# Half-wide products that alternate between the two partition halves of their output

## The chip, the core and the metric

The kernel runs on one core of a Trainium2 chip. The metric is the device time of one execution in microseconds (us). The engines are named as the profile names them: PE (TensorE, the matrix products), PEld (its weight loads, which overlap PE), DVE (VectorE), ACT (ScalarE), POOL (GpSimd) and SP (SyncE, which issues most transfers).

## The reference, cut to what matters

Two blocks follow each other over 512 tokens of 1024 features. Block 1 has two mixers and two feed-forward layers; its second mixer holds a spatial gating and a causal "forgetting" attention, both with 8 heads of 64 features. Block 2 has two layers, each with three branches; branch c is a neighbourhood attention with 8 heads of 64 features, for 512 tokens and, in layer 0, also for 256 tokens of a context. All of it is in float32.

```python
# block 1, second mixer
mixed = jnp.einsum('gts,bnsgc->bntgc', w_causal, gv) + b_s.T[:, :, None]     # c: 64 features of a gating head
...
p = jax.nn.softmax(logits, axis=-1)
return jnp.einsum('bhqk,bhkd->bhqd', p.astype(v.dtype), v)                    # d: 64 features of a head
# block 2, branch c
return jnp.einsum('bhnqik,binkhd->bnqhd', p_loc, vr) + jnp.einsum('bhnqj,bjhd->bnqhd', p_ctx, vc)
...
y_cc = softmax_attn(na_h(cqc), na_h(ckc), na_h(cvc)).reshape(B, L, BR_W) * jax.nn.silu(czc)
```

## The kernel before

Features lie on partitions and tokens on the free axis. The projections are products of 128 weight columns with 512 or 256 tokens; each float32 weight is split into two parts (tiles `wh`, `wl`) and each operand into two (`H`, `L`), and three passes of the split type stand for one float32 product. Weights come in units of 128 columns through `wload`: a transfer on SP, a copy on ACT, a subtraction on DVE.

The 64-feature heads are treated in pairs (`hp` 0 and 1, the first and the second head of pair `j`). For a tile `t` of 128 queries `attend` makes the scores (`mm_stack`), the softmax on DVE and ACT, the transposes of the probabilities (PE, `P<-C,..` in the trace, C being the constants with the identity), their copy out of PSUM into `pT` (ACT), and then the product with the head's values. That last product has 64 output features: head 0 writes partitions 0 to 63 of its PSUM tile, head 1 writes partitions 64 to 127. It is a plain float32 product with 128 rows, 64 weight columns and 128 moving columns, one for each tile `n` of keys, summed in PSUM. In this text these are the half-wide products; one that writes partitions 0 to 63 belongs to half 0, the others to half 1. The spatial gating (`mixed`) has the same shape: head `2 j` in half 0, head `2 j + 1` in half 1, four products each. There are 400 half-wide products: 112 in block 1 (80 of the attention, 32 of the gating), 160 in layer 0 of block 2, 128 in layer 1. A float32 product leaves two matmul records and two weight-load records in the trace, so there are 800 records.

The order on the engines isn't that of the code: the class `Order` records the instructions, and `flush` issues them by a list schedule, engine by engine, from planned costs. An engine takes the first written instruction that can start. So the half-wide products of one head are placed one by one, in between projections and transposes, and stretches of them of any length and of either half arise. All instructions of the kernel are issued at one line of `flush`, so the trace has them all at L465 and they are told apart by their tiles and shapes. In the names P is PSUM; `t` tiles belong to block 1 and `s` tiles to block 2; `P<-t,t` with the shape 128*64 is a half-wide product of block 1, `P<-s,s` with 128*64 one of block 2.

Of the kernel before, what the change touches and what calls it, by code (L numbers as in the profile page):

```python
# [12 lines left out]
AF = mybir.ActivationFunctionType  # L13
# [14 lines left out]
# ---------------------------------------------------------------- host layout  # L28
def _units(w):
    """[K, N] -> [N/128, 128, K/128, 128]: each 128-column unit contiguous."""  # L30
    k, n = w.shape
    return np.ascontiguousarray(w.reshape(k // 128, 128, n // 128, 128).transpose(2, 1, 0, 3))


def _halves(w):
    """[K, N] -> [2, 128, K/256, N]: a unit of N columns in two halves of K."""
    k, n = w.shape
    return np.ascontiguousarray(w.reshape(2, k // 256, 128, n).transpose(0, 2, 1, 3))


def _cols(v):
    """[.., C] -> [128, n]: a feature vector as partition columns, leading axes in order."""
    v = np.asarray(v)
    return v.reshape(-1, 128).T
# [17 lines left out]
def consts():  # L62
# [4 lines left out]
    # queries on partitions, keys on the free axis  # L67
    p.add("cmask", np.where(i[None, :] <= i[:, None], 0.0, NEG).astype(np.float32))
    # source s on partitions, target t on the free axis
# [7 lines left out]
def rope_tables():  # L77
    """[2, 128, 512]: cos and signed sin, a feature on each partition (two groups of 64)."""
# [3 lines left out]
    ang = np.concatenate([row[:, None] * inv, col[:, None] * inv], axis=-1)  # [T, 32]  # L82
# [10 lines left out]
def nbias(rpb):  # L93
    """[H, 15, 31] -> [H, 128, 768]: the bias of a block of 16 columns x 8 rows of queries
    against its window of 32 columns x 8 rows of keys, for the first, a middle and the last
    block; keys outside a query's own window get a constant."""
    out = []
    r = np.arange(8)
    for n in (0, 1, 3):
# [6 lines left out]
        b = rpb[:, ri[None, :, None, :], ci[:, None, :, None]]  # H, qc, rq, kc, rk  # L106
# [41 lines left out]
def layout(inputs):  # L148
# [28 lines left out]
    for l in range(2):  # L177
# [5 lines left out]
        # [8 m, 3 branches, 128, 4, 128]  # L183
# [6 lines left out]
# ---------------------------------------------------------------- issue order  # L190
# [9 lines left out]
class Order:  # L200
    """Records the instructions of a stretch of the kernel in the order they are written in, and
    issues them in the order of a list schedule: an engine takes the first written one of those
    that can start, given when operands arrive and slots of tile tags come free. Tile puts in the
    waits and the addresses."""

# [6 lines left out]
    # sets of function tables; the others are in all of them  # L212
# [3 lines left out]
    def __init__(self, tc, nc):  # L216
# [8 lines left out]
        self.tiles = {}   # name -> [tag, number]  # L225
        self.caps = {}    # tag -> slots
        self.made = {}    # tag -> tiles made
        self.clock = {e: 0.0 for e in self.LAG}
        self.dma = 0.0
        self.slots = {}   # tag -> times at which free slots came free  # L230
        self.held = {}    # tile -> tag, while it holds a slot
        self.done_at = {}  # tile -> end of its last issued instruction
        self.reset()

    def reset(self):
        self.ops = []
        self.floor = 0.0  # the earliest start of the next ones
        self.late = 0     # how many instructions later the next ones may come
        self.acc = {}
        self.last = {}  # L240

# [10 lines left out]
    # ---- recording  # L252
# [13 lines left out]

    def record(self, eng, op, f, a, k):
# [9 lines left out]
        i = len(self.ops)  # L277
        deps = {}
        if eng == "pe":
            # accumulation groups in a PSUM bank follow one another  # L280
            x = k["out"] if "out" in k else a[0]
            bank = (x.tensor.name, x.offset % (list(x.ap)[0][0] or 1) // 512)
            if k.get("start", True) and bank in self.last:
                deps[self.last[bank]] = False
# [26 lines left out]
        self.ops.append(dict(p=(i + self.late, i), r=self.floor, e=eng, s=self.SETS.get(a[2]) if eng == "act" and op == "activation" else None, f=f, a=a, k=k, d=deps, t=touched, c=self._cost(eng, op, a, k, aps, psum)))  # L311
# [37 lines left out]
    # ---- issue  # L349
    def flush(self, keep=()):  # L350
# [20 lines left out]
        # tiles of each tag that wait for a slot, in the order they were made  # L371
# [90 lines left out]
        with self.tc.manual_schedule():  # L462
            for i in order:
                o = ops[i]
                o["f"](*o["a"], **o["k"])  # L465
        self.reset()


def weave(*gens):
    """Runs generators, of (steps, generator) each, side by side in proportion to their lengths."""  # L470
# [8 lines left out]
def chain(*gens):  # L479
    """the same, one after another"""  # L480
# [6 lines left out]
# ---------------------------------------------------------------- the kernel  # L487
class Kern:
    WST = 3

    def __init__(self, ctx, tc, A, cat, vat):
# [15 lines left out]
        # the split operand of the projections, tokens of x first, then those of the context  # L507
# [23 lines left out]
    def pt(self, n=512, p=128):  # L531
        """a bank of PSUM"""
# [3 lines left out]
    def pts(self, n, p=128):  # L536
        """n columns over banks of PSUM: (tile, first column, columns)"""
        return [(self.pt(min(512, n - o), p), o, min(512, n - o)) for o in range(0, n, 512)]

    # ---- weights: loaded in 128-column units and split exactly into two float32r parts  # L540
# [16 lines left out]
    def mm3(self, ps, w, xh, xl, order=None, start=True, stop=True):  # L557
        """ps += w.T x over the k tiles of xh, xl (lists), as three float32r passes."""
# [8 lines left out]
    def tok4(self, src, tiles):  # L567
        """a projection of about 256 columns of each 128-column tile of H, L (their columns in
        `tiles`): the first tile, [128 tokens, tile, columns], with as many to a bank of PSUM as fit"""
# [20 lines left out]
    def stack(self, q, k, hp, new, nq, nk):  # L590
        """Operands on all 128 rows for the product of a head's 64 rows of q and k:
        [q hi; q hi], [q lo; q lo] against [k hi; k lo]."""
# [19 lines left out]
    # ---- 1/sqrt(v) for few columns  # L612
# [17 lines left out]
class Stream:  # L630
    """The running sum of squares of a residual stream's features, for n tokens."""
# [16 lines left out]
    def sums(self, p):  # L648
        """the sums, tokens on partitions, into columns of PSUM"""
# [7 lines left out]
    def spread(self, r, p):  # L657
        """a value for each token, on every partition, into PSUM"""
# [6 lines left out]
    def rstd(self):  # L665
        """1/rms of each token: on every partition, in PSUM, and with tokens on partitions"""
# [12 lines left out]
def block1(K, X, out, dbg, mods, B, es):  # L679
# [18 lines left out]
    def feed(m, g):  # L698
        """X[:, m] g as operand of the next projections, whose results get the factor 1/rms"""
# [10 lines left out]
    def proj(*src):  # L710
        """one or two units of 128 columns"""
# [7 lines left out]
    def scaled(p, R):  # L719
        """halves of a PSUM tile, each times R"""  # L720
# [5 lines left out]
    def gelu2(src, dst=None):  # L726
        """2 gelu(src), the tanh form."""
# [10 lines left out]
    def conv(p, wname, bname, j, taps, ntile):  # L738
        """causal depthwise convolution of a [128, T] tile"""
# [15 lines left out]
    def lru_rates():  # L755
        """4 softplus(-lambda) and its negative; half biases"""
# [24 lines left out]
    def even(first):  # L781
# [11 lines left out]
        for j in range(0, 4, 2):  # L793
            for j, p in zip((j, j + 1), scaled(proj(W[j], W[j + 1]) if j else pre, R)):
# [10 lines left out]
                # 1 - a^2 = tanh(z) (1 + a^2)  # L805
# [30 lines left out]
    def odd():  # L836
# [4 lines left out]
        # forget gates: negative running sum of log sigmoid, one row per head  # L841
# [27 lines left out]
        # spatial gating: gate half, token-major  # L869
# [13 lines left out]
        def mixed():  # L883
            # gt holds 2 gelu
# [13 lines left out]
            for j in range(4):  # L898
                m = K.pt(T)
                for q in range(2):  # L900
                    h = 2 * j + q
                    for n in range(4):
                        nc.tensor.matmul(m[64 * q:64 * q + 64, n * 128:(n + 1) * 128],
                                         lhsT=gt[n][:, h * 64:(h + 1) * 64], rhs=wt[h // 4][:, h % 4],
                                         start=True, stop=True)
                mx.append(t2())
# [5 lines left out]
        # forgetting attention, two heads at a time  # L912
# [37 lines left out]
        def attend(j):  # L950
            vt, st, cb, cm = heads.pop(j)
            o = K.pt(T)
            for t in range(4):
                q0, nk = t * 128, (t + 1) * 128
                for hp in range(2):
                    P0 = 64 * hp
# [22 lines left out]
                    pT = t2()  # L979
                    nc.scalar.activation(pT[:, :nk], tt[:, :nk], AF.Copy)  # L980
                    for n in range(t + 1):
# [847 lines left out]
```

## Time and profile before

| | |
|---|---|
| three runs | 2955.85, 2951.63, 2955.36 us; median 2955.36 us |
| span of the profiled execution, first to last instruction | 2953.9 us |
| PE busy | 2902.0 us (98% of the span) |
| DVE, ACT, POOL busy | 1889.7, 1256.5, 242.5 us (64%, 43%, 8%) |
| mean granted clock of PE | 0.994 of full speed |

The profiled execution's own time isn't listed apart from its span; the median of the runs lies 1.5 us above that span. A share of busy time is read with care on PE: its records overlap, since matmuls are pipelined. What a product costs PE is read from the distance between the starts of two that follow each other, or from the length of a row that merges many of them.

### The profile page before, as it was taken

How to read it: one execution, taken by the hardware profiler on the slowest of the kernel's cores; microseconds unless marked ns; L12 is line 12 of the kernel's file. 1: busy time of each engine (PE TensorE's matmuls, PEld its weight loads, DVE VectorE, ACT ScalarE, POOL GpSimd, SP SyncE). 2: the span in 40 equal slices, each digit the busy share in tenths (PEclk: the TensorE clock that was granted, in tenths of full speed). 3: DMA queues.
4: the chain of work that ended last, by engine and by line, in shares of the span. 5: the costliest groups of instructions: out<-in, count | busy, mean ns of one | idle time of the engine just before them, and what ended most of it. 6: DMA issues, size and time to landing. Idle time of an engine off the chain costs nothing.

```text
span 2953.9 us, 41015 instructions
## 1 busy us (share of the span) xinstructions
PE 2902.0 (98%) x15990; PEld 2458.0 (83%) x15990; DVE 1889.7 (64%) x3799; ACT 1256.5 (43%) x2400; POOL 242.5 (8%) x184
## 2 busy tenths in 40 slices
PE   9999999999999999999999999999999999999998
PEld 6888888887888888888888888888888888888887
DVE  7778687568885876556876763222475586765334
ACT  6344244454442444655555432222356554533223
POOL 1010000100100011001110210000300011110002
PEclk9999999999999999999999999999999999999999
DMA  4333433322334433111111111222422111222333
GB/s 153 126 119 120 145 132 108 118 81 72 127 109 146 144 91 127 47 63 44 37 45 58 54 61 54 68 65 67 136 79 82 37 58 44 73 72 68 100 93 104
DMA packets 94802, 260.58 MB, mean 88 GB/s; under 512 B 9608, under 2 KB 23304, under 8 KB 94608
## 3 DMA queue, kind: packets, MB, share of 16 engines
q1 hardware_dynamic: 94464, 257.96, 27.0%
q8 instruction: 125, 2.05, 0.3%
q14 instruction: 69, 0.57, 0.1%
q10 hardware_dynamic: 144, 0.00, 0.0%
HBM read 251.29 MB, written 6.64 MB: 87 GB/s over the span
## 4 chain that ended last, share of the span: by engine, by line
PE 93%; DVE 4%; ACT 1%; issue 1%; DMA 1%; POOL 0%; SPq 0%; POOLq 0%; ACTq 0%; DVEq 0%
PE P L465 93%; DVE s L465 2%; DVE wl L465 1%; ACT s L465 1%; DVE tn L465 1%; DVE t L465 0%; DMA s<-cmd 0%; POOL s L465 0%; ACT t L465 0%; ACT wh L465 0%; DMA V<-in_vec 0%; DMA t<-cd 0%; DVE L L465 0%; DMA ws<-in_w0in 0%; DMA cmd<-s 0%
## 5 line engine op out<-in xcount | busy, mean ns | idle before, releaser
L465 PE MATMUL P<-L,wh 128*128 128x512 f32 (+1 forms) x2936 | 1079.7, 368 | 3.7 <-DVE L L465 3.6
L465 PE MATMUL P<-H,wh 128*128 128x512 f32 (+1 forms) x2936 | 1078.4, 368 | 3.7 <-ACT s L465 1.6
L465 PE MATMUL P<-H,wl 128*128 128x512 f32 (+1 forms) x2936 | 1078.3, 367 | 3.3 <-DVE wl L465 3.3
L465 ACT ACTIVATE wh<-ws 128x1024 fp32r<-128x1024 f32 (+4 forms) x426 | 412.1, 968 | 926.2 <-PE P L465 836.9
L465 DVE TENSOR_TENSOR wl<-ws,wh 128x1024 fp32r<-128x1024 f32 (+4 forms) x426 | 484.8, 1139 | 461.4 <-ACT wh L465 447.6
L465 PEld LDWEIGHTS P<-H,wh 128*128 128x128 f32 x2936 | 553.2, 188 | 101.7 <-ACT s L465 2.5
L465 PEld LDWEIGHTS P<-L,wh 128*128 128x128 f32 x2936 | 553.1, 188 | 100.9 <-DVE L L465 5.7
L465 PEld LDWEIGHTS P<-H,wl 128*128 128x128 f32 x2936 | 553.5, 189 | 99.1 <-DVE wl L465 4.6
L465 ACT ACTIVATE s<-P 128x512 f32<-128x512 f32 (+2 forms) x486 | 217.7, 478 | 334.1 <-PE P L465 332.4
L465 PE MATMUL P<-t,wh 128*128 128x512 f32 x960 | 301.7, 395 | 0.3 <-ACT t L465 0.3
L465 PE MATMUL P<-s,s 128*128 128x256 f32 (+4 forms) x2112 | 283.7, 290 | 13.2 <-DVE s L465 10.0
L465 PEld LDWEIGHTS P<-s,s 128*128 128x128 f32 (+1 forms) x2112 | 251.3, 178 | 39.8 <-DVE s L465 11.7
L465 POOL TENSOR_TENSOR s<-s,s 128x512 f32<-128x512 f32 (+2 forms) x87 | 116.5, 1348 | 1277.5 <-DVE s L465 852.1
L465 PEld LDWEIGHTS P<-t,wh 128*128 128x128 f32 x960 | 180.5, 188 | 42.6 <-ACT t L465 0.6
L465 PE MATMUL P<-t,wl 128*128 128x512 f32 x480 | 189.5, 395 | 0.0
L465 ACT ACTIVATE s<-s 64x768 fp32r<-64x768 f32 (+7 forms) x162 | 109.2, 680 | 125.2 <-DVE s L465 112.2
L465 DVE TENSOR_REDUCE tn<-P 128x1 f32<-128x512 f32 (+1 forms) x224 | 105.8, 493 | 79.0 <-PE P L465 78.6
L465 DVE TENSOR_TENSOR s<-s,s 128x512 f32<-128x512 f32 (+7 forms) x168 | 145.2, 867 | 17.5 <-ACT s L465 12.3
L465 PE MATMUL P<-s,wh 128*128 128x512 f32 (+1 forms) x576 | 155.0, 356 | 0.0
L465 DVE SCALAR_TENSOR_TENSOR t<-t,V,t 128x511 f32<-128x511 f32 (+1 forms) x196 | 148.0, 761 | 3.2 <-ACT t L465 1.4
L465 PE MATMUL P<-wl,H 128*128 128x256 f32 (+2 forms) x512 | 145.6, 285 | 0.0
L465 PE MATMUL P<-wh,L 128*128 128x256 f32 (+2 forms) x512 | 145.5, 284 | 0.0
(136 smaller groups left out, 3015.1 us busy)
## 6 DMA issues: line engine op xcount, KB each, us to landing
ws<-in_w2in SPq DMA_DIRECT2D x136, 512.0 KB, 3.3
ws<-in_up SPq DMA_DIRECT2D x88, 512.0 KB, 3.3
wm<-in_w_mod SPq DMA_DIRECT2D x48, 512.0 KB, 4.6
ws<-in_down SPq DMA_DIRECT2D x32, 384.0 KB, 3.2
ws<-in_w2br SPq DMA_DIRECT2D x48, 256.0 KB, 2.6
ws<-in_down SPq DMA_DIRECT2D x32, 320.0 KB, 2.9
ws<-in_w0in SPq DMA_DIRECT2D x18, 512.0 KB, 3.8
ws<-in_w2out SPq DMA_DIRECT2D x16, 512.0 KB, 3.5
```

Of the source, the lines that this page charges most:

```text
L465: o["f"](*o["a"], **o["k"])
```

## The change

`Order` gets two calls, `together` and `apart`. PE instructions that are recorded between them become one entry of the schedule, which waits for the operands of all of them and is issued in one piece, in the order in which they are written. The half-wide products are now written in that way: for each tile `n` first the product of half 0, then that of half 1. So in the attentions the products of head 0 no longer follow head 0's transposes; they stand with those of head 1, after both heads' probabilities are transposed and copied, and two `pT` tiles are held at a time. The number of products and their shapes stay as they are. Nothing else in the computation changes (the other lines of the diff drop comments, which leaves the issuing lines at L486 for the first product of a piece and L488 for its others).

```diff
+    def together(self):
+
+        self.run = -1
+
+    def apart(self):
+        self.run = None
...
+        joins = self.run is not None and eng == "pe"
+        if joins:
+            if self.run >= 0:
+                i = self.run
+            self.run = i
...
-            if k.get("start", True) and bank in self.last:
+            if k.get("start", True) and self.last.get(bank, i) != i:
...
+        if i < len(self.ops):
+            o = self.ops[i]
+            o["more"].append((f, a, k))
+            o["c"] += self._cost(eng, op, a, k, aps, psum)
+            o["t"] |= touched
+            for j, raw in deps.items():
+                o["d"][j] = o["d"].get(j, False) or raw
+            return
...
+                for f, a, k in o["more"]:
+                    f(*a, **k)
...
-                for q in range(2):
-                    h = 2 * j + q
-                    for n in range(4):
+                nc.together()
+                for n in range(4):
+                    for q in range(2):
+                        h = 2 * j + q
                         nc.tensor.matmul(m[64 * q:64 * q + 64, n * 128:(n + 1) * 128],
                                          lhsT=gt[n][:, h * 64:(h + 1) * 64], rhs=wt[h // 4][:, h % 4],
                                          start=True, stop=True)
+                nc.apart()
...
-                    pT = t2()
-                    nc.scalar.activation(pT[:, :nk], tt[:, :nk], AF.Copy)
-                    for n in range(t + 1):
-                        nc.tensor.matmul(o[P0:P0 + 64, q0:nk], lhsT=vt[:, n, P0:P0 + 64],
-                                         rhs=pT[:, n * 128:(n + 1) * 128], start=(n == 0), stop=(n == t))
+                    pT.append(t2())
+                    nc.scalar.activation(pT[hp][:, :nk], tt[:, :nk], AF.Copy)
+                    if hp:
+
+                        nc.together()
+                        for n in range(t + 1):
+                            for P0 in (0, 64):
+                                nc.tensor.matmul(o[P0:P0 + 64, q0:nk], lhsT=vt[:, n, P0:P0 + 64],
+                                                 rhs=pT[P0 // 64][:, n * 128:(n + 1) * 128], start=(n == 0), stop=(n == t))
+                        nc.apart()
...
-                    for i in range(nb):
+                    pT.append(self.s(512))
+                    self.copy(pT[hp], self.transposes(L[hp], [c0 + i * 128 for i in range(nb)]))
...
+                nc.together()
+                for i in range(nb):
+                    for P0 in (0, 64):
                         nc.tensor.matmul(O[P0:P0 + 64], lhsT=v_[i][:, P0:P0 + 64],
-                                         rhs=pT[:, i * 128:(i + 1) * 128], start=(i == 0), stop=(i == nb - 1))
+                                         rhs=pT[P0 // 64][:, i * 128:(i + 1) * 128], start=(i == 0), stop=(i == nb - 1))
+                nc.apart()
```

Counted over the whole order of PE, with a for a product of half 0 and b for one of half 1, in the order in which they stand; a stretch is a run of half-wide products with nothing else between them:

| | stretches before | stretches now |
|---|---|---|
| block 1 | 32, of 1 to 25 products: aa 5, bb 4, aaa 4, bbb 3, aaaa 3, bbbb 3, b 3, a 2, and five longer or mixed | 16: ab 3, abab 4, ababab 4, abababab 3, one of 5 pairs, one of 16 (the gating) |
| layer 0 | 24: aaaabbbb 13, aabb 7, and four others | 22: abababab 13, abab 7, one of 6 pairs, one of 8 |
| layer 1 | 16: aaaabbbb 16 | 16: abababab 16 |

The first place is PE in block 1, head pair 0, query tile 3 (PSUM tile P_958; t_1043 holds the transposed probabilities of head 0 and t_1054 those of head 1, t_921 the values; P_1044 and P_1074 are projections). Before, head 0's four products stand here as soon as they can, and head 1's four stand 67 rows further on:

```order
L465 MATMUL P_1044<-wl_1021,H 128x256
L465 MATMUL P_958<-t_1043,t_921 64x128 x4
L465 MATMUL P_1044<-wh_1020,H 128x256
...
L465 MATMUL P_1074<-wh_1072,H 128x256
L465 MATMUL P_958<-t_1054,t_921 64x128 x4
L465 MATMUL P_1064<-C,t_1059 128x128
```

Now all eight stand at the second of these places:

```order
L486 MATMUL P_1074<-wl_1073,H 128x256
L486 MATMUL P_1074<-wh_1072,H 128x256
L486 MATMUL P_958<-t_1043,t_921 64x128
L488 MATMUL P_958<-t_1054,t_921 64x128
...
L486 MATMUL P_1064<-C,t_1059 128x128
L486 MATMUL P_1074<-wh_1072,L 128x256
```

Between the two rows of P_958 that are shown and the transpose the same pair stands three times more. Two stretches of four became one of four pairs, and head 0's products moved behind the projections that stood between.

The second place is PE in layer 0 of block 2, head pair 0, the context's two query tiles (PSUM tiles P_9747 and P_9761; s_9748 and s_9762 belong to head 0, s_9750 and s_9764 to head 1, s_9669 holds the values; `P<-C,..` are transposes, P_9766 is a projection). Before:

```order
L465 MATMUL P_9763<-C,s_9756 128x128
L465 MATMUL P_9747<-s_9748,s_9669 64x128 x2
L465 MATMUL P_9747<-s_9750,s_9669 64x128 x2
L465 MATMUL P_9763<-C,s_9756 128x128
L465 MATMUL P_9765<-C,s_9759 128x128 x2
...
L465 MATMUL P_9766<-H,wl_2066 128x512
L465 MATMUL P_9761<-s_9762,s_9669 64x128 x2
L465 MATMUL P_9761<-s_9764,s_9669 64x128 x2
L465 MATMUL P_9766<-H,wh_2065 128x512
```

Now:

```order
L486 MATMUL P_9766<-H,wl_2066 128x512
L486 MATMUL P_9747<-s_9748,s_9669 64x128
L488 MATMUL P_9747<-s_9750,s_9669 64x128
...
L486 MATMUL P_9766<-H,wh_2065 128x512
L486 MATMUL P_9766<-L,wh_2065 128x512
L486 MATMUL P_9763<-C,s_9756 128x128 x2
L486 MATMUL P_9765<-C,s_9759 128x128 x2
```

Where rows are left out the same pair stands once more. The stretch kept its length and its two halves; the order within it went from aabb to abab, and it stands between projections, ahead of the transposes that it stood among.

## Rows read from the trace of the kernel before

**Rows 1.** The page: span, and busy time with share and instructions by engine.

```profile
span 2953.9 us, 41015 instructions
PE 2902.0 (98%) x15990; PEld 2458.0 (83%) x15990; DVE 1889.7 (64%) x3799; ACT 1256.5 (43%) x2400; POOL 242.5 (8%) x184
```

**Rows 2.** The page: the chain that ended last, shares of the span by engine.

```profile
PE 93%; DVE 4%; ACT 1%; issue 1%; DMA 1%; POOL 0%; SPq 0%; POOLq 0%; ACTq 0%; DVEq 0%
```

**Rows 3.** Windows of block 1's attention and branch c, layers 0 and 1.

```profile
core 0: us, PE busy (x) PEld busy (x) DVE busy (x) ACT busy (x) POOL busy (x), PEclk, DMA share, GB/s
600.00:732.00 132.00, 131.75 (x820) 107.41 (x820) 90.80 (x282) 69.37 (x151) 9.33 (x8) 0.99 0.24 80
1192.00:1380.00 188.00, 186.65 (x1350) 164.40 (x1348) 106.29 (x289) 109.23 (x275) 5.11 (x4) 1.00 0.15 52
2207.00:2353.00 146.00, 146.00 (x995) 126.60 (x993) 88.19 (x234) 87.36 (x214) 5.21 (x4) 1.00 0.19 63
```

**Rows 4.** PE's waits in the first two windows of rows 3 (total, times, longest).

```profile
PE P L465 <- ACT t L465: 0.3, 1, 0.3
...
PE P L465 <- DVE s L465: 1.4, 1, 1.4
```

**Rows 5.** Half-wide products by shape, in these three windows (count, busy us, mean ns, idle).

```profile
L465 PE MATMUL P<-t,t 128*64 128x128 f32 x224 | 29.2, 285 | 0.0
...
L465 PE MATMUL P<-s,s 128*64 128x128 f32 x320 | 30.7, 280 | 0.0
...
L465 PE MATMUL P<-s,s 128*64 128x128 f32 x256 | 25.3, 279 | 0.0
```

**Rows 6.** Timeline of PE, block 1, around aaaa at 611.51 (start, length, records).

```profile
611.18 0.28 PE L465 MATMUL P<-wh,L 128*128 128x256 f32 x1
611.30 0.28 PE L465 MATMUL P<-wl,H 128*128 128x256 f32 x1
611.51 1.09 PE L465 MATMUL P<-t,t 128*64 128x128 f32 x8
612.53 0.38 PE L465 MATMUL P<-wh,H 128*128 128x256 f32 x1
612.75 0.28 PE L465 MATMUL P<-wh,L 128*128 128x256 f32 x1
612.87 0.28 PE L465 MATMUL P<-wl,H 128*128 128x256 f32 x1
```

**Rows 7.** Timeline of PE, block 1: two products of one half.

```profile
702.73 0.65 PE L465 MATMUL P<-t,t 128*64 128x128 f32 x4
```

**Rows 8.** Timeline of PE, layer 0: the context's two stretches aabb.

```profile
1208.35 0.74 PE L465 MATMUL P<-s,s 128*64 128x128 f32 x8
1209.02 0.55 PE L465 MATMUL P<-C,s 128*128 128x128 f32 x3
...
1210.19 0.67 PE L465 MATMUL P<-s,s 128*64 128x128 f32 x8
```

**Rows 9.** Timeline of PE, layer 0: aaaabbbb and aaaabbbbaaaa.

```profile
1196.12 1.58 PE L465 MATMUL P<-s,s 128*64 128x128 f32 x16
1197.63 1.64 PE L465 MATMUL P<-C,s 128*128 128x128 f32 x13
1199.19 2.08 PE L465 MATMUL P<-s,s 128*64 128x128 f32 x24
```

**Rows 10.** Window of block 1 in which DVE is fullest.

```profile
660.00:680.00 20.00, 20.00 (x99) 15.71 (x98) 18.43 (x62) 13.25 (x28) 0.00 (x0) 1.00 0.24 80
```

**Rows 11.** The page: ACT's copies out of PSUM in block 2 (count, busy us, mean ns, idle).

```profile
L465 ACT ACTIVATE s<-P 128x512 f32<-128x512 f32 (+2 forms) x486 | 217.7, 478 | 334.1 <-PE P L465 332.4
```

More of the change, by code (lines that the diff above doesn't have):

```diff
@@ L265, in _region @@
         return p0, p0 + dims[0][1], lo, hi + 1
+    def together(self):
+        self.run = -1
+    def apart(self):
+        self.run = None
     def record(self, eng, op, f, a, k):
@@ L310, in record @@
             self.acc[name] = keep
-        self.ops.append(dict(p=(i + self.late, i), r=self.floor, e=eng, s=self.SETS.get(a[2]) if eng == "act" and op == "activation" else None, f=f, a=a, k=k, d=deps, t=touched, c=self._cost(eng, op, a, k, aps, psum)))
+        if i < len(self.ops):
[6 more added lines that the diff above has]
+            return
+        self.ops.append(dict(more=[], p=(i + self.late, i), r=self.floor, e=eng, s=self.SETS.get(a[2]) if eng == "act" and op == "activation" else None, f=f, a=a, k=k, d=deps, t=touched, c=self._cost(eng, op, a, k, aps, psum)))
     @staticmethod
@@ L954, in attend @@
                 q0, nk = t * 128, (t + 1) * 128
+                pT = []
                 for hp in range(2):
-                    P0 = 64 * hp
                     s = K.pt()
@@ L1625, in attend @@
                 O = K.pt(128)
+                pT = []
                 for hp in range(2):
-                    P0 = 64 * hp
                     nc.vector.tensor_scalar(L[hp][:, c0:], L[hp][:, c0:], rs[:, hp:hp + 1], None, op0=ALU.mult)
-                    pT = self.s(512)
-                    self.copy(pT, self.transposes(L[hp], [c0 + i * 128 for i in range(nb)]))
-                    v_ = (va[:, 4], va[:, 5])
-                    if isl:
-                        v_ = {0: (va[:, 0], va[:, 1]), 1: (vb[:, 0], vb[:, 1]), 2: (vb[:, 1], vb[:, 2]),
-                              3: (va[:, 2], va[:, 3])}[t] + v_
-                    for i in range(nb):
+                    pT.append(self.s(512))
+                    self.copy(pT[hp], self.transposes(L[hp], [c0 + i * 128 for i in range(nb)]))
+                v_ = (va[:, 4], va[:, 5])
+                if isl:
+                    v_ = {0: (va[:, 0], va[:, 1]), 1: (vb[:, 0], vb[:, 1]), 2: (vb[:, 1], vb[:, 2]),
+                          3: (va[:, 2], va[:, 3])}[t] + v_
+                nc.together()
+                for i in range(nb):
+                    for P0 in (0, 64):
                         nc.tensor.matmul(O[P0:P0 + 64], lhsT=v_[i][:, P0:P0 + 64],
-                                         rhs=pT[:, i * 128:(i + 1) * 128], start=(i == 0), stop=(i == nb - 1))
+                                         rhs=pT[P0 // 64][:, i * 128:(i + 1) * 128], start=(i == 0), stop=(i == nb - 1))
+                nc.apart()
                 nc.scalar.activation(o[:, t * 128:(t + 1) * 128], O, AF.Copy, scale=0.5)
```

## The prediction

> **What bounds the kernel.** I read the page first. The span is 2953.9 us and PE is busy for 2902.0 us of it, DVE for 1889.7 [rows 1]; of the chain that ended last 93% is PE [rows 2]. A busy share alone says little on PE, whose records overlap, so I went to the three stretches of the program that hold the half-wide products: block 1's second mixer, and branch c of the two layers of block 2. There PE is busy for 131.75 of 132 us, 186.65 of 188 and 146.00 of 146, while DVE has 90.80, 106.29 and 88.19 and ACT no more than 109.23 [rows 3]. The list of waits says the same from the other side: PE waited for 0.3 us in the first, for 1.4 us in the second [rows 4], and for nothing in the third. So in these 466 us PE never stands still for data, and what its instructions cost there is what the kernel pays. The reader should see that this is a case in which a shorter PE instruction stream should shorten the run by as much, until some other engine becomes late.
>
> **What the half-wide products cost now.** Their rows, merged to busy time, are 29.2 us in block 1, 30.7 us in layer 0 and 25.3 us in layer 1 [rows 5]: together 85.2 us. The timeline shows how one stretch gets its length. Two products of one half (4 records) last 0.65 us [rows 7], four of one half (8 records) 1.09 us [rows 6]. The difference is 0.44 us for 4 records: 0.11 us a record, 0.22 us a product, and 0.21 us that a stretch has once, however long it is.
>
> Now both halves. Four products aabb, two for each half, last 0.67 us, and in one case 0.74 us [rows 8]; there are seven such stretches, six of them with the first length. That is 0.02 and 0.09 us more than two products of one half alone. So the two halves run beside each other nearly all the time, and the second half is almost free. Eight products aaaabbbb last 1.58 us [rows 9]. One after the other they would take 0.21 + 8 x 0.22 = 1.97 us, side by side 0.21 + 4 x 0.22 = 1.09 us; they get 0.39 of the 0.88 us that could be had. What I take from this is that PE starts half 1 while records of half 0 are still ahead of it, but only when few are: with two products ahead nearly all overlaps, with four about half. The twelve products aaaabbbbaaaa in 2.08 us [rows 9] fit: 2.85 us one after the other, so two changes of half gave 0.77, again 0.39 each.
>
> **What the change does to that, step by step.** (1) Order. In a pair ab only one product stands ahead of each product of the other half, which is less than in aabb. If the halves run side by side, a stretch of k pairs lasts 0.21 + 0.22 k plus a small offset of half 1. The near rows for the offset are 0.02 (six of seven) and 0.09 (one of seven): 0.03 on average, which I take. The far end is one record, 0.11 us, if half 1's first record must wait until both of half 0's first product have started. The program now has 54 stretches with 200 pairs in all (the table with the diff). So their length is 54 x (0.21 + 0.03) + 200 x 0.22 = 13.0 + 44.0 = 57.0 us, against 85.2 us: 28.2 us less. With an offset of 0.02 it is 56.4 us (28.8 less), with 0.11 it is 61.3 us (23.9 less).
>
> (2) Fewer stretches, 54 for 72. What entering and leaving costs stands around the stretch at 611.51 [rows 6]. The product ahead of it has 0.21 us to itself (611.30 to 611.51), where its neighbours have 0.12; that is 0.09 more. The next product starts at 612.53, 0.07 us ahead of the stretch's end at 612.60, so 0.07 is to be taken off; and it has 0.22 us to itself instead of 0.12, 0.10 more. Together 0.12 us for each stretch, beside its length. 18 fewer are worth 2.2 us.
>
> (3) Head 0's products come later, since they wait for head 1's probabilities. I put this at nothing. In block 1 some 67 rows of projections stood between the two and are still there to fill PE (the first place shown); in block 2 the two heads' transposes already stood side by side. Head 1's products waited for just the same copy before, and PE's waits came to 1.7 us in all [rows 4]. If the cover were gone, each of the 54 stretches would show PE idle for one copy by ACT, 0.48 us [rows 11], 26 us in all.
>
> (4) The order on the other engines is all but the same: POOL's is unchanged, and those of SP, ACT and DVE have a few instructions swapped near the moved products. No transfer, copy or reduction is added. Nothing is charged for it; PE's work covers it as long as DVE and ACT have idle time in these windows [rows 3].
>
> The sum is 28.2 + 2.2 = 30.4 us: 13.0 + 1.9 of it in block 1, the rest in branch c. The span of the profiled execution would go from 2953.9 to 2923.5 us. The median of the runs is 1.5 us above that span, so I set the time at 2955.4 - 30.4 = 2925 us.
>
> **The rivals.** *Given back in block 1.* PE gets faster in the 132 us of the first window, and in the fullest 20 us there DVE is already busy for 18.43 us [rows 10]. If DVE's chain through softmax and gating sets the pace once PE is ahead, PE waits for it, and block 1's share of 14.9 us is lost: 2925 + 15 = 2940 us. For it: this window. Against it: over the whole 132 us DVE has 41 us idle [rows 3], and PE has its projections to do meanwhile. 8 in 100.
>
> *The change doesn't do what it says.* The overlap in aabb might belong to short stretches alone, so that a long alternating one gains no more than the blocks did. Then the 85.2 us stay and only the 18 entries are saved: 2953 us. For it: no long stretch of before alternates product by product. Against it: aaaabbbbaaaa overlapped at both of its changes. 4 in 100.
>
> *Slower: the halves take turns.* Every product would then wait for the one written ahead of it, in whatever half, and alternation would take away even the overlap that there is. All 400 products cost 0.22 us: 54 x 0.21 + 400 x 0.22 = 99.3 us, 14.1 more than now, less the 2.2 of the entries: 12 us slower, 2967 us. It is decided by the price of a pair. Above (87.4 - 13.0) / 200 = 0.37 us the change loses; my forecast has 0.22, turns would be 0.44. For it: a block of four doesn't overlap in full, so PE doesn't choose freely among its queue. Against it: 1.58 us for aaaabbbb and 0.67 us for aabb [rows 8, 9] can't be had in turns (1.97 and 1.09). 5 in 100.
> A rule of the Trainium skill speaks for this rival (TensorE: Matmul & The Clock Gate, Part 3, "The mechanism"): weight loads overlap running products only where the row groups differ, and products start strictly in the order written. Both halves here use all 128 rows, so by that rule the sum would be that of turns, 99.3 us; by the rows it is 57.0. The trace doesn't agree with the rule as far as it goes: under it the 16 records of aaaabbbb would last 1.97 us, and the row has 1.58. So it raises the chance only a little.
>
> **How the numbers follow.** The forecast has 83 in 100. Its own range goes from the two offsets (2924 to 2929) and the scatter of the runs shown (4 us below the median, under 1 above) to 2920 to 2930. To leave out no more than 2 in 10 the range takes in the first rival: 2919 to 2941. What a measurement of this kernel can tell from no change is about 0.2%, 6 us. Forecast and first rival are both faster by more than that: 0.91; the second is within it: 0.04; the third is slower: 0.05.
>
> **What would show it.** In the timeline of after, abababab (16 records) should last 1.12 us and abab (8 records) 0.68 us, the gating's 16 pairs 3.76 us; in turns abababab has 1.97, with the blocks' overlap 1.58. The busy time of the 128*64 shapes should sum to 57 us, with the first product of a stretch and the others on lines of their own. PE's waits in the three stretches should stay near 2 us; if they grow to 15 us behind DVE in block 1, it is the first rival. The stretch lengths outside these three windows should be as before; the prediction is wrong for another reason if the half-wide products shrink as said and the span doesn't, and then the time must stand as new waits of PE in the projections that follow.

## The result and the profile after

The changed kernel takes 2926.34 us (median of 4 runs, 2926.07 to 2929.05) against 2953.88 us for the kernel before beside it (4 runs, 2951.63 to 2955.85). The ratio is 0.9911, with a 95% interval of 0.9899 to 0.9923. The forecast was 2925 us, range 2919 to 2941. The profiled execution took 2929.05 us with a span of 2927.2 us.

The page of the changed kernel: span, busy time by engine, and the chain that ended last.

```profile
span 2927.2 us, 41030 instructions
...
PE 2874.2 (98%) x15990; PEld 2433.7 (83%) x15990; DVE 1887.6 (64%) x3799; ACT 1256.0 (43%) x2400; POOL 243.7 (8%) x184
...
PE 92%; DVE 4%; ACT 1%; issue 1%; DMA 1%; POOL 0%; SPq 0%; POOLq 0%; ACTq 0%; DVEq 0%
```

Against [rows 1, 2] the span is 26.7 us shorter and PE's busy time 27.8 us, with the same 15990 matmul records. PE's idle time, span less busy time, went from 51.9 to 53.0 us. DVE, ACT and POOL did the same work in the shorter span. So the saving is PE's own. The 1.1 us more of idle time are less than what two executions of one kernel differ by (53.0 us here, 55.3 in f1_changed below), so where they arise has to be read from the places themselves.

The same instructions are now split over two lines: L486 issues the first product of a piece, L488 the others. The timeline of PE in layer 1 shows the first stretch abababab between its neighbours (start, length, records):

```profile
2190.41 0.40 PE L486 MATMUL P<-H,wh 128*128 128x512 f32 x1
2190.74 0.32 PE L486 MATMUL P<-s,s 128*64 128x128 f32 x1
2190.74 0.32 PE L488 MATMUL P<-s,s 128*64 128x128 f32 x1
2190.90 0.27 PE L486 MATMUL P<-s,s 128*64 128x128 f32 x1
2190.91 0.93 PE L488 MATMUL P<-s,s 128*64 128x128 f32 x13
2191.76 1.09 PE L486 MATMUL P<-C,s 128*128 128x128 f32 x8
```

The first two records of a stretch, one of each half, start within 0.01 us, and so do the next two. The stretch lasts from 2190.74 to 2190.91 + 0.93 = 2191.84, 1.10 us. The same sixteen records lasted 1.58 us as aaaabbbb [rows 9], and 1.10 us is within 0.01 of what eight records of one half alone took [rows 6]. A context's stretch abab of layer 0 in the same view:

```profile
1193.69 0.32 PE L486 MATMUL P<-s,s 128*64 128x128 f32 x1
1193.70 0.32 PE L488 MATMUL P<-s,s 128*64 128x128 f32 x1
1193.85 0.27 PE L486 MATMUL P<-s,s 128*64 128x128 f32 x1
1193.86 0.49 PE L488 MATMUL P<-s,s 128*64 128x128 f32 x5
```

It lasts 0.66 us, as aabb did before at its best (0.67 us, [rows 8]) and as two products of one half did alone [rows 7]. The gating's 32 products are one stretch from 683.38 to 687.10 us, 3.72 us, where 3.76 was forecast; of its rows these are the first and the last:

```profile
683.38 0.32 PE L486 MATMUL P<-t,t 128*64 128x128 f32 x1
...
686.17 0.93 PE L488 MATMUL P<-t,t 128*64 128x128 f32 x13
```

The windows of the three places, which answer to [rows 3], with the columns of that view:

```profile
600.00:720.00 120.00, 118.51 (x825) 99.16 (x824) 92.57 (x290) 69.38 (x153) 9.77 (x8) 0.99 0.27 93
1180.00:1365.00 185.00, 183.65 (x1380) 161.05 (x1379) 110.09 (x298) 111.10 (x280) 5.13 (x4) 1.00 0.16 54
2188.00:2330.00 142.00, 142.00 (x1021) 122.20 (x1020) 88.96 (x240) 89.28 (x220) 5.23 (x4) 1.00 0.19 65
```

PE is as full in branch c as it was (1.35 and 0.00 us idle in these windows, as in [rows 3]). In block 1 it now has 1.5 us idle, where 0.25 us stood before. The timeline there shows 1.1 us of it at the end of the mixer, at the last head pair's last tile (idle time and what ended it in brackets):

```profile
715.52 0.43 PE L486 MATMUL P<-t,t 128*64 128x128 f32 x2
716.34 1.09 PE L488 MATMUL P<-t,t 128*64 128x128 f32 x14 [0.38 <-ACT t L486]
718.12 1.22 PE L486 MATMUL P<-t,wh 128*128 128x512 f32 x4 [0.69 <-ACT t L486]
```

The first product of head 0 starts; the next, of head 1, waits for ACT to copy its probabilities; then the output projection waits for ACT's copy of the finished heads. These are step 3's waits, at the one place where no projection is left to fill them; before, PE waited for 0.3 us there [rows 4]. They also show what a piece is on the engine: the schedule plans it for when all its operands are there, but each product still waits for its own. The other 0.4 us are a wait for DVE earlier in the mixer.

### The profile page after: what moved, and what is told of

Same layout as the page of the kernel before. It is cut to its first block, busy times and chain, and to the rows that moved or that the text cites. A ratio compares the mean times of both kernels' runs of the same rounds, so it can differ in the third digit from the quotient of the medians.

```text
span 2927.2 us, 41030 instructions
## 1 busy us (share of the span) xinstructions
PE 2874.2 (98%) x15990; PEld 2433.7 (83%) x15990; DVE 1887.6 (64%) x3799; ACT 1256.0 (43%) x2400; POOL 243.7 (8%) x184
## 4 chain that ended last, share of the span: by engine, by line
PE 92%; DVE 4%; ACT 1%; issue 1%; DMA 1%; POOL 0%; SPq 0%; POOLq 0%; ACTq 0%; DVEq 0%
PE P L486 91%; DVE s L486 2%; PE P L488 1%; DVE wl L486 1%; DVE t L486 1%; DVE tn L486 1%; ACT s L486 1%; DMA s<-cmd 0%; POOL s L486 0%; ACT t L486 0%; DVE L L486 0%; ACT wh L486 0%; DMA V<-in_vec 0%; DMA t<-cd 0%; DMA ws<-in_w0in 0%
## 5 line engine op out<-in xcount | busy, mean ns | idle before, releaser
L486 PE MATMUL P<-L,wh 128*128 128x512 f32 (+1 forms) x2936 | 1080.1, 368 | 4.2 <-DVE L L486 3.8
L486 PE MATMUL P<-H,wh 128*128 128x512 f32 (+1 forms) x2936 | 1079.2, 368 | 3.6 <-ACT s L486 1.6
L486 PE MATMUL P<-H,wl 128*128 128x512 f32 (+1 forms) x2936 | 1078.8, 368 | 2.2 <-DVE wl L486 2.2
L486 ACT ACTIVATE wh<-ws 128x1024 fp32r<-128x1024 f32 (+4 forms) x426 | 412.7, 970 | 922.1 <-PE P L486 827.7
L486 DVE TENSOR_TENSOR wl<-ws,wh 128x1024 fp32r<-128x1024 f32 (+4 forms) x426 | 484.5, 1138 | 450.2 <-ACT wh L486 436.3
L486 PEld LDWEIGHTS P<-L,wh 128*128 128x128 f32 x2936 | 553.7, 189 | 101.6 <-DVE L L486 6.4
L486 PEld LDWEIGHTS P<-H,wh 128*128 128x128 f32 x2936 | 553.7, 189 | 101.1 <-ACT s L486 2.5
L486 PEld LDWEIGHTS P<-H,wl 128*128 128x128 f32 x2936 | 553.9, 189 | 97.6 <-DVE wl L486 3.5
L486 ACT ACTIVATE s<-P 128x512 f32<-128x512 f32 (+2 forms) x486 | 217.6, 479 | 320.1 <-PE P L486 297.1
L486 PE MATMUL P<-t,wh 128*128 128x512 f32 x960 | 301.3, 395 | 0.7 <-ACT t L486 0.7
L486 PE MATMUL P<-s,s 128*128 128x128 f32 (+4 forms) x1616 | 244.1, 292 | 13.3 <-DVE s L486 9.8
L486 PEld LDWEIGHTS P<-s,s 128*128 128x128 f32 (+1 forms) x1616 | 211.6, 189 | 39.4 <-DVE s L486 11.5
L486 POOL TENSOR_TENSOR s<-s,s 128x512 f32<-128x512 f32 (+2 forms) x87 | 116.6, 1350 | 1263.1 <-DVE s L486 848.0
L486 PEld LDWEIGHTS P<-t,wh 128*128 128x128 f32 x960 | 180.5, 188 | 42.9 <-ACT t L486 0.9
L486 PE MATMUL P<-t,wl 128*128 128x512 f32 x480 | 189.4, 395 | 0.0
L486 ACT ACTIVATE s<-s 64x768 fp32r<-64x768 f32 (+7 forms) x162 | 109.4, 681 | 125.8 <-DVE s L486 112.0
L486 DVE TENSOR_TENSOR s<-s,s 128x512 f32<-128x512 f32 (+7 forms) x168 | 145.2, 868 | 17.1 <-ACT s L486 12.0
L486 PE MATMUL P<-s,wh 128*128 128x512 f32 (+1 forms) x576 | 155.7, 357 | 0.0
L486 DVE TENSOR_REDUCE tn<-P 128x1 f32<-128x512 f32 (+1 forms) x224 | 106.1, 493 | 76.2 <-PE P L486 75.6
L486 DVE SCALAR_TENSOR_TENSOR t<-t,V,t 128x511 f32<-128x511 f32 (+1 forms) x196 | 148.2, 762 | 3.2 <-ACT t L486 1.3
L486 ACT ACTIVATE t<-t 128x512 f32<-128x512 f32 (+4 forms) x162 | 98.0, 612 | 114.0 <-DVE t L486 113.4
L486 PE MATMUL P<-wh,H 128*128 128x256 f32 (+2 forms) x512 | 145.8, 285 | 0.0
```

## The experiments

Times are medians. The first four ran on one chip beside the kernel before at 2952.28 us (23 runs, 2949.04 to 2956.68), the other four on one chip beside it at 2952.81 us (9 runs, 2950.08 to 2957.71).

| run | us | ratio to before, 95% interval | span | PE busy | span less busy |
|---|---|---|---|---|---|
| e1_blocks | 2942.82 | 0.9966, 0.9955 to 0.9977 | 2939.8 | 2888.3 | 51.5 |
| e2_free | 2949.05 | 0.9990, 0.9981 to 0.9999 | 2946.6 | 2893.8 | 52.8 |
| e3_onehalf | 2955.29 | 1.0010, 1.0001 to 1.0019 | 2955.2 | 2903.2 | 52.0 |
| e4_twotiles | 2925.24 | 0.9901, 0.9888 to 0.9915 | 2919.0 | 2864.1 | 54.9 |
| f1_changed | 2927.18 | 0.9909, 0.9895 to 0.9923 | 2928.3 | 2873.0 | 55.3 |
| f2_twotiles | 2922.99 | 0.9897, 0.9884 to 0.9911 | 2924.0 | 2868.7 | 55.3 |
| f3_twos | 2924.85 | 0.9906, 0.9892 to 0.9920 | 2929.2 | 2874.6 | 54.6 |
| f4_block1 | 2941.39 | 0.9959, 0.9945 to 0.9973 | 2938.5 | 2885.9 | 52.6 |

The last column is what to look at first. Over kernels whose spans differ by 36 us PE's idle time stays between 51.5 and 55.3 us; it was 51.9 before. What moves with the kernel is how long PE is busy.

**e1_blocks: the same pieces, half by half.**

```diff
-                for i in range(nb):
-                    for P0 in (0, 64):
+                for P0 in (0, 64):
+                    for i in range(nb):
                         nc.tensor.matmul(O[P0:P0 + 64], lhsT=v_[i][:, P0:P0 + 64],
```

(and so in block 1's attention and gating)

> The changed kernel with the pieces kept, but each written half by half: all products of half 0, then all of half 1 (aaaabbbb where it has abababab). Number and place of the stretches are those of the changed kernel. Theory (alternation lets the halves run side by side): aaaabbbb lasts 1.58 us again as in the kernel before, against 1.10 us in the changed one, aabb stays at 0.67; summed over the 54 stretches some 18 us more, about 2944 us, and the half-wide products' busy time goes from 57 to about 75 us. Rival (the gain is that of whole pieces and of another order around them): about 2926 us, no difference from the changed kernel.

Measured 2942.82 us; 0.9966 against 0.9911 for the changed kernel. PE in layer 1 of this kernel, one stretch aaaabbbb and its neighbours:

```profile
2321.25 0.28 PE L486 MATMUL P<-H,wh 128*128 128x256 f32 x1
2321.46 0.43 PE L486 MATMUL P<-s,s 128*64 128x128 f32 x2
2321.73 1.31 PE L488 MATMUL P<-s,s 128*64 128x128 f32 x14
2322.97 0.39 PE L486 MATMUL P<-L,wh 128*128 128x256 f32 x1
```

From 2321.46 to 2323.04: 1.58 us again. Summed over all stretches, with records that overlap counted once, the half-wide products keep PE busy for 75.5 us, where 75 were expected and the changed kernel has 57.0. The place and the number of the stretches are those of the changed kernel, so of the changed kernel's 0.89% (26 us) 0.55% (16 us) are the alternation itself, and 0.34% (10 us) remain for pieces in blocks: fewer stretches, and both heads always together. The theory stands.

**e2_free: alternating as written, but every product an entry of its own.**

```diff
     def together(self):
 
-        self.run = -1
+        self.run = None
```

> The changed kernel with the half-wide products written in alternation, but each an entry of its own in the schedule, so that it may start as soon as it can. The order then has 104 stretches for 54: mostly a single product of one half that goes ahead, and then bababab. Theory: a lone product costs 0.43 us of length and 0.12 us of entry and exit, 0.55 us, and the rest of the stretch is as long as before, so 50 more stretches cost some 27 us: about 2953 us, no better than the kernel before. Rival (alternation is all that matters, pieces are not needed): the long part of each stretch still overlaps, a few us at most: 2926 to 2932 us.

Measured 2949.05 us. The schedule lets head 0's first product go as soon as it can, ahead of the others. A timeline of layer 1 of this kernel shows the pattern that repeats, a lone product and then bababab:

```profile
2345.41 0.43 PE L486 MATMUL P<-s,s 128*64 128x128 f32 x2
2345.77 0.39 PE L486 MATMUL P<-wh,H 128*128 128x256 f32 x1
2345.99 0.28 PE L486 MATMUL P<-wh,L 128*128 128x256 f32 x1
2346.11 0.28 PE L486 MATMUL P<-wl,H 128*128 128x256 f32 x1
2346.32 1.09 PE L486 MATMUL P<-s,s 128*64 128x128 f32 x14
```

The lone product has 0.43 us as reckoned, and the seven that follow need 1.09 us, as long as eight. So alternation in the code is worth little (0.1%) where the schedule may pull the products apart; the piece is needed. The cost was put 4 us too high: 23 us over the changed kernel by the two ratios, not 27.

**e3_onehalf: both heads in half 0, in two banks (branch c).**

```diff
-                O = K.pt(128)
+                O = [K.pt(128) for _ in range(2)]
...
-                        nc.tensor.matmul(O[P0:P0 + 64], lhsT=v_[i][:, P0:P0 + 64],
+                        nc.tensor.matmul(O[P0 // 64][:64], lhsT=v_[i][:, P0:P0 + 64],
...
-                nc.scalar.activation(o[:, t * 128:(t + 1) * 128], O, AF.Copy, scale=0.5)
+                for hp in range(2):
+                    nc.scalar.activation(o[64 * hp:64 * hp + 64, t * 128:(t + 1) * 128], O[hp][:64], AF.Copy, scale=0.5)
```

> The changed kernel, but in branch c (288 of the 400 products, 38 of the 54 stretches) both heads write partitions 0 to 63, each in a bank of its own, and the copy on ACT is done in two parts that put them back in place. The order of the products is the same pair by pair. Theory (two halves of the output run side by side, one half takes turns): 8 products last 0.21 + 8 x 0.22 = 1.97 us for 1.10, 4 last 1.09 for 0.66, in all some 31 us more: about 2957 us. Rival (what helps is that two accumulators alternate, whatever their half): stretch lengths as in the changed kernel, about 2926 us; the extra copies on ACT are hidden in either case.

Measured 2955.29 us, 29 us over the changed kernel by the two ratios. In layer 1 of this kernel the 16 records of a piece last from 2347.63 to 2349.59, 1.96 us, as the timeline of PE shows:

```profile
2347.63 0.43 PE L486 MATMUL P<-s,s 128*64 128x128 f32 x2
2347.90 1.69 PE L488 MATMUL P<-s,s 128*64 128x128 f32 x14
2349.52 0.39 PE L486 MATMUL P<-wh,H 128*128 128x256 f32 x1
```

The prediction's third rival, the halves taking turns, priced this at 1.97. The same order of the same products costs 0.86 us more when both heads write the same partitions, although their banks differ. The halves are what runs side by side. It also shows what "turns" would have made of branch c: it is 14.9 us slower than in the kernel before, and block 1, which still alternates, is 12.6 us faster, so that of the whole gain nothing is left (times between the same products, as in the table below).

**f3_twos: two of each half in turn, in one piece.**

```diff
-                for i in range(nb):
-                    for P0 in (0, 64):
+                for i0 in range(0, nb, 2):
+                    for P0, i in [(P0, i) for P0 in (0, 64) for i in (i0, i0 + 1)]:
                         nc.tensor.matmul(O[P0:P0 + 64], lhsT=v_[i][:, P0:P0 + 64],
```

(and so in block 1)

> The changed kernel with the same pieces, written two products of half 0, two of half 1, and so on (aabbaabb for abababab). Theory (PE starts the other half as long as no more than about two products of the first stand ahead of it; what failed in aaaabbbb was only the distance): the stretches last as long as alternating ones, 1.10 to 1.17 us for aabbaabb, 2926 to 2929 us. Rival (only single alternation runs side by side over a whole stretch): aabbaabb lies between 1.10 and the 1.58 us of aaaabbbb, by a fifth or more of that distance, and the time is 2930 to 2943 us.

Measured 2924.85 us, no different from the changed kernel. PE in layer 1 of this kernel:

```profile
2196.16 0.32 PE L486 MATMUL P<-s,s 128*64 128x128 f32 x1
2196.17 0.32 PE L488 MATMUL P<-s,s 128*64 128x128 f32 x1
2196.32 0.27 PE L486 MATMUL P<-s,s 128*64 128x128 f32 x1
2196.33 0.97 PE L488 MATMUL P<-s,s 128*64 128x128 f32 x13
```

aabbaabb lasts 1.14 us, 0.04 more than abababab. Two products ahead are next to no hindrance; four are (e1_blocks), and so are three: aaabbb in block 1 of e1_blocks lasts 1.15 us (608.23 + 0.88 less 607.96), where ababab has 0.88 in the changed kernel.

```profile
607.96 0.43 PE L486 MATMUL P<-t,t 128*64 128x128 f32 x2
608.23 0.88 PE L488 MATMUL P<-t,t 128*64 128x128 f32 x10
```

What decides is how far ahead in the order the other half's next product stands.

**f4_block1: the change in block 1 alone.** Branch c is written as in the kernel before:

```diff
...
-                nc.together()
-                for i in range(nb):
-                    for P0 in (0, 64):
+                    for i in range(nb):
                         nc.tensor.matmul(O[P0:P0 + 64], lhsT=v_[i][:, P0:P0 + 64],
-                                         rhs=pT[P0 // 64][:, i * 128:(i + 1) * 128], start=(i == 0), stop=(i == nb - 1))
-                nc.apart()
+                                         rhs=pT[:, i * 128:(i + 1) * 128], start=(i == 0), stop=(i == nb - 1))
```

> The change in block 1 alone (attention and gating), branch c written as in the kernel before. Theory (PE's savings add up, stretch by stretch): block 1 has 13.0 us of length and 1.9 us of entries, so 13 to 15 us below the kernel before, about 2938 us. Rival (the first of the prediction: block 1's share is lost to DVE, which is fullest there): less than 8 us below, 2945 us or more, with PE's waits on DVE grown in block 1's window.

Measured 2941.39 us, 11 us below the kernel before by the medians; 13 to 15 were expected, and the rival allowed less than 8. PE's waits in block 1 of this kernel, from 605 to 725 us (total, times, longest):

```profile
PE P L486 <- ACT t L486: 0.7, 1, 0.7
PE P L486 <- DVE t L486: 0.4, 1, 0.4
PE P L488 <- ACT t L486: 0.4, 1, 0.4
```

DVE accounts for 0.4 us, so block 1's share isn't lost to it. The two waits on ACT, 1.1 us together, are those at the end of the mixer shown above. Between the same products ahead of and behind block 1's mixer the profiled execution is 12.8 us shorter than before, and branch c takes what it took (0.0 us apart in both layers). PE's busy time is 16.1 us below [rows 1]; what goes beyond the 12.8 us stands outside the three places. So the time is some 2 us short of what was expected, about half of it the waits that are new.

**f1_changed, e4_twotiles, f2_twotiles: longer pieces.** The changed kernel again, and one that holds two query tiles of branch c and issues both in one piece, 20 stretches for 38 there:

```diff
+                held.append((t, O, pT, v_))
+                if t % 2:
+                    nc.together()
+                    for _, Ou, pu, vu in held:
+                        for i in range(nb):
+                            for P0 in (0, 64):
+                                nc.tensor.matmul(Ou[P0:P0 + 64], lhsT=vu[i][:, P0:P0 + 64],
+                                                 rhs=pu[P0 // 64][:, i * 128:(i + 1) * 128], start=(i == 0), stop=(i == nb - 1))
+                    nc.apart()
...
```

> The changed kernel with two query tiles in one piece in branch c: 20 stretches of 8 or 4 pairs there for 38 of 4 or 2. Theory: each stretch that goes takes 0.24 us of its own length and 0.12 us of entry and exit with it, 18 x 0.36 = 6.5 us: about 2920 us. Rival (a piece that waits for two tiles' probabilities makes PE wait, since banks and tiles are held longer): a wait of one copy, 0.48 us, at each of the 20 pieces or more, about 2930 us or slower, and it shows in PE's waits on ACT in the two windows of branch c.

> The changed kernel once more, as the measure for the three others on the same chip: 2926 us by the first measurement, within 2 us.

> The kernel with two query tiles in one piece in branch c again, now beside the changed kernel on one chip. Theory (each of the 18 stretches that go takes 0.36 us with it): 5 to 6.5 us below the changed kernel, 2920 us. Rival (longer pieces give it back in waits): within 2 us of the changed kernel.

The first time it took 2925.24 us (2920.81 to 2925.47). Beside the changed kernel on one chip it took 2922.99 us against 2927.18. A piece of 8 pairs lasts 1.96 us in layer 1 (from 2230.02 to 2231.98), where two of 4 pairs take 2.20:

```profile
2230.02 0.32 PE L486 MATMUL P<-s,s 128*64 128x128 f32 x1
2230.02 0.32 PE L488 MATMUL P<-s,s 128*64 128x128 f32 x1
2230.18 0.27 PE L486 MATMUL P<-s,s 128*64 128x128 f32 x1
2230.18 1.80 PE L488 MATMUL P<-s,s 128*64 128x128 f32 x29
```

The medians of the whole program differ by 4.2 us, but the two intervals overlap (0.9884 to 0.9911 and 0.9895 to 0.9923), so by the runs alone it is likely and not shown that it is faster than the changed kernel. In branch c it is: between the same products both of its profiled executions are 3.6 to 3.7 us shorter than both of the changed kernel's, 1.1 us of it in layer 0 and 2.5 to 2.6 in layer 1. That is less than the 6.5 us expected. In layer 1 the 8 stretches that went gave 0.32 us each. In layer 0 the rival has its part. PE's waits there, from 1175 to 1365 us, were a single one of 1.4 us on DVE in the changed kernel. With two tiles in one piece they are, in both executions (total, times, longest):

```profile
PE P L486 <- DVE s L486: 2.9, 4, 1.4
PE P L486 <- ACT s L486: 0.2, 1, 0.2
```

That is 1.7 us more, mostly behind DVE and not behind ACT as the rival had it. Against the kernel before, two tiles in one piece are faster by 1.0%.

## Why the prediction was right

**What bounds the kernel.** Right, and the table shows it best: PE's idle time hardly moves in any of the kernels, whatever PE's work takes. Where the saving stands can be read by place. The order of PE outside the three places is that of before, so the time from one product ahead of a place to one behind it can be compared. The table has by how much it is shorter than in the kernel before, in us, in the profiled executions; the forecast is the prediction's sum, split by its own counts of stretches and pairs.

| | forecast | changed kernel | f1_changed | f4_block1 | e4_twotiles, f2_twotiles |
|---|---|---|---|---|---|
| block 1 | 14.9 | 12.4 | 13.6 | 12.8 | 13.0, 12.7 |
| layer 0 | 8.1 | 8.0 | 8.0 | 0.0 | 9.1, 9.1 |
| layer 1 | 7.4 | 7.6 | 7.7 | 0.0 | 10.2, 10.3 |
| everywhere else | 0 | -1.4 | -3.7 | 2.5 | 2.6, -2.2 |

**Step 1, the length of stretches.** Right to about 0.02 us a stretch: 1.10, 0.66 and 3.72 us where 1.12, 0.68 and 3.76 were forecast, since the offset of the other half is 0.01 us and not the 0.03 that was taken. The bound of 0.11 for PE keeping to the written order wasn't met. The busy time of the half-wide products fell from 85.2 to 57.0 us, the very number forecast (56.6 in f1_changed); that it fits to the tenth is luck, for the smaller offset is made up by a few longer stretches, among them the one that waits at the end of the mixer and one at 600 us, where the granted clock fell (1.05 us, and 0.66 in f1_changed, where it didn't). e3_onehalf and e1_blocks show the two prices on which the step rested, 1.96 and 1.58 us.

**Step 2, entries.** Somewhat too much. In layer 1 of the kernel with two query tiles a stretch that went was worth 0.32 us where 0.36 were reckoned; 0.22 of it is the length that the half-wide products lost there ((17.5 - 15.7) / 8), so 0.10 is left for entry and exit, not 0.12. In block 1, 16 stretches fewer were put at 1.9 us; the 12.4 and 12.8 us of the table, less the 12.6 us by which the half-wide products got shorter there and with the 1.2 us of new idle time added back, leave 1.0 and 1.4 us.

**Step 3, head 0's products later.** Put at nothing. At the end of block 1's mixer, where the cover of projections runs out, PE waits for 1.1 us where it waited for 0.3 before. The 0.4 us behind DVE are new too, which makes 1.2 us with them; whether the order or the fuller DVE is their cause no run separates. Over the three places PE's waits come to 2.9 us, where the prediction expected near 2.

**The sum.** 30.4 us were forecast, 27.5 measured between the medians (26.7 in span). Branch c came out as forecast, by the table 15.6 us for 15.5. Block 1 is 2.5 us short: 1.2 us are the new waits, 0.9 the entries, 0.4 the length. The other 1.4 us stand where the instructions are the same, and f1_changed, which is the same kernel, lost 3.7 us there: this is scatter between executions. Part of it is where the granted clock falls. In the profiled execution of the changed kernel it fell at the end of block 1, in that of f1_changed it didn't, with the same idle time of PE; the one before fell near 2379 us, which the changed kernel didn't (first row the changed kernel, then f1_changed, then the kernel before):

```profile
1140.00:1150.00 10.00, 8.38 (x32) 6.32 (x31) 9.79 (x15) 5.27 (x9) 0.00 (x0) 0.83 0.07 26
1140.00:1150.00 10.00, 8.37 (x37) 6.36 (x36) 9.56 (x15) 5.49 (x9) 0.00 (x0) 1.00 0.07 26
2375.00:2385.00 10.00, 8.09 (x39) 6.62 (x38) 8.75 (x23) 7.55 (x23) 2.11 (x2) 0.83 0.00 1
```

PE had been idle for 1.62 us in the first 10 us and for 1.63 in the second. Between the same products the first fall cost the changed kernel 1.5 us, and the last cost the kernel before 1.5 us, so these two cancel. The other three runs of the changed kernel, with a mean granted clock of 0.996 against 0.994, took 2926.1 to 2926.5 us, some 2.6 us less than the profiled one. That the time came within 1.3 us of the forecast although the saving was 2.9 us short is in part luck: the forecast started from 2955.36 us, the median of three runs of the kernel before, and with the fourth it is 2953.88.

**The rivals.** *Given back in block 1*: fell with f4_block1, whose waits on DVE there are 0.4 us. *Doesn't do what it says*: fell with e1_blocks, where the same pieces without alternation are 16 us slower. A row of the kernel before that the prediction didn't show spoke against it already: twelve records in block 1 last 0.88 us, the price of three pairs side by side (0.21 + 3 x 0.22), where six products in turns would take 1.53.

```profile
689.66 0.88 PE L465 MATMUL P<-t,t 128*64 128x128 f32 x12
```

*Turns*: fell with the 1.10 us of abababab; e3_onehalf is what it would have looked like in branch c. The rule of the Trainium skill that was cited for it (TensorE: Matmul & The Clock Gate, Part 3, "The mechanism"), that products start strictly in the written order and loads overlap running products only where row groups differ, doesn't describe these runs: in e1_blocks the sixteen records of aaaabbbb last 1.58 us where that order would give 1.97, and in the changed kernel both halves, with the same 128 rows, need no more time than one. Nor do the records start in the written order there: the first of the second product (L488) starts at 2190.74, the second record of the first product (L486) at 2190.90.

## What to carry to other kernels

Products whose outputs take only one half of the partitions are worth pairing with others that take the other half, and placing next to each other in the order: here a pair then cost what one did, 0.22 us. The order within a stretch matters down to about two products; a scheduler that issues each product as soon as it can undoes it, so the group has to be one entry for it. Look for the proof in the trace of before: a stretch in which both halves happened to stand close had the forecast's price already.

## What the runs showed of the hardware that was not expected

How far PE looks ahead can be read from three orders of the same sixteen records: aaaabbbb 1.58 us, aabbaabb 1.14, abababab 1.10, and 1.96 with one half alone. Four products of a half standing ahead of the other half lose more than half of the overlap, two lose almost nothing. Each change of half between blocks of four gave 0.39 us, one change or two [rows 9].

The reach can also be counted in records. In block 1 of e1_blocks a piece aaaabbbb is followed at once by a piece ab:

```profile
690.24 0.43 PE L486 MATMUL P<-t,t 128*64 128x128 f32 x2
690.50 0.98 PE L488 MATMUL P<-t,t 128*64 128x128 f32 x11
691.22 0.32 PE L486 MATMUL P<-t,t 128*64 128x128 f32 x1
691.33 0.27 PE L488 MATMUL P<-t,t 128*64 128x128 f32 x1
```

The second piece's first product, of half 0 (L486 at 691.22), starts when 13 of the 16 records written ahead of it have started: three are still to come. The first record of a half that starts afresh is 0.32 us long, the others 0.27, and by that sign it is three everywhere: in all 29 stretches aaaabbbb of the kernel before half 1 starts as the sixth record, 0.49 us after the first, with three of half 0's eight to come, and in the four aaabbb of e1_blocks as the fourth, 0.28 us after the first. From there the other half takes its own time, which gives the lengths: 0.49 + 1.09 = 1.58 and 0.28 + 0.88 = 1.16 (1.15 in the row shown). So in these runs PE passes over three records, a product and a half, to start one of the other half; whether it is as many with other shapes no run shows.
